# A 2-layer gMLP/mLSTM decoder step: where one weight split stands on VectorE, and five transposes instead of six for a head's values

## The chip, the core and the metric

The kernel runs on one core of one Trainium2 chip. The metric is device time in microseconds of one execution of the whole program. TensorE (PE in the profile) multiplies matrices and transposes; VectorE (DVE), ScalarE (ACT) and GpSimd (POOL) do the elementwise work; SyncE (SP) issues all DMAs of this kernel, in one queue. Matmul results go to PSUM, which has eight banks of 512 float32 columns on 128 partitions; everything else is in SBUF.

## The reference

One inference step of a decoder with two layers, on 256 prompt tokens and on 8 sequences of 8 new sample tokens (64 tokens), together 320 columns. Each layer is a mixer and a gated MLP with a causal convolution; layer 0 mixes by chunked spatial gating, layer 1 by an mLSTM with 8 heads, key width 128 and value width 256. The change touches layer 1, whose mixer computes per head

```python
p = x @ w_in                       # q, k (through a causal convolution and silu), v, o, gates
sc = einsum('bhtd,bhsd->bhts', qc, kc) * w_intra
num = w_inter[..., None] * einsum('bhtd,bhde->bhte', qc, C) + einsum('bhts,bhse->bhte', sc, vc)
h = num / maximum(abs(den), exp(-m_t))[..., None]
C_new = decay[..., None, None] * C + einsum('bhsd,bhse->bhde', kg, vc)
hn = (h - mean(h)) * rsqrt(var(h) + EPS) * gn_g
y = (sigmoid(o_pre) * hn) @ w_out
```

The outputs are y for all tokens, and the new states, among them C for the prompt and for each of the eight sample sequences.

## The kernel before

**Precision.** Every float32 operand of a matmul is split into a high part that TensorE's fast float32 form (fp32r) holds exactly enough, and a low part, the rest: names end in `h` and `l`. A product takes three matmuls: high by high, low by high, high by low. For each weight chunk of 128 x 1024 (`raw`), ScalarE writes the high part `wh` (L154) and VectorE the low part `wl = raw - wh` (L155).

**Weights.** A list fixes the order of all weight chunks. `take` (called once for each chunk that TensorE uses) sees to it that four chunks further on are being loaded (`AHEAD`), and that one chunk further on is split (`SPLIT_AHEAD`), by calling `prefetch(n, m)`: load until n chunks are loaded, split until m are split. `raw` has four buffers, `wh` and `wl` three each. `block` multiplies eight chunks of rows into one PSUM tile `pm`; in layer 1 all products with `wh` come first, then those with `wl`.

**Order.** Matmuls and transposes are pinned to program order (`mm`, `tr`). The instructions of the other engines are placed by a scheduler, which may move an instruction ahead of others of its engine where its inputs allow; `tc.issue_after(x)` keeps what is issued inside it behind instruction x. PSUM is used through two pools, `psm` with three banks (tag `pm`) and `psa` with five (tag `pa`).

**The heads.** The loop over `h` at the end of `layer_b` interleaves head `h` with the rest of head `h - 1`. For `h` from 1 on TensorE runs the six blocks of head `h` (q, k, v, v, o, o), and between them, of head `h - 1`: the product of the queries with the old states (`inter`, tile `num`, with the split states `Ch` and `Cl`), the numerator (`numer`), the new prompt state (`state_prompt`), and in four pieces the new sample states (`state_sample`, tile `pcs`, then `C` on VectorE, then the store `out_Cs`); then the scores of head `h` (`scores`, tile `psc`). After the last block come

- `finish(h - 1)`: for each half `e` of the 256 value columns, three transposes of the normalised output `hn` into `phn`, then `y_b = (tanh + 1) * phn` on VectorE (L1027), then its high part `yhb` on ScalarE (L1029) and its low part `ylb` on VectorE (L1030), with the gain;
- `state_sample(h - 1, 3)`;
- `k_nat(h)`: three transposes of k into `pk`, from which `kgs` (sample) and `kgh`, `kgl` (prompt) are made; `kgs`, masked per sequence on GpSimd, is `kgz`;
- `v_nat(h)`: transposes of v into `pv`, see below;
- `inter(h, 0)`, whose first matmul opens a new PSUM tile `num`; then the splits of two more states.

With `rows_in(h)` at the top of the loop the load of `Mb` (one row of gate weights, spread over the partitions) is issued; `w`, the exponentials of the gates, read it on ScalarE (L811). From head 4 on the loop also runs the first half of the output projection (`early`), which adds blocks of matmuls with little work on the other engines. `o_b` (L1013) is the scaled o block, and `qk_epi` makes `bpad`, the convolution `bcv` (one instruction on ScalarE, three on VectorE), `bth`, `qs` and their parts `qh`, `qhl`, `kh`, `khl`.

**The values.** v comes out of the blocks with channels on partitions and tokens on columns, one `pm` for each half `e`. `v_epi` copies it to `vTb`: 320 columns, and the 64 sample columns once more behind them, so that columns 256 to 383 hold the sample's tokens twice. `v_nat` transposes three groups of 128 columns of both halves, six transposes; in the third group the sample's 64 tokens so stand on partitions 0 to 63 and again on 64 to 127. ScalarE writes the high part `vh[:, t]` of each group from PSUM with the tokens' scale (L851), VectorE the low part (L854): for the prompt's two groups to `vl`, for the sample's to partitions 64 to 127 of `vh[:, 2]`, over the second copy, so that one matmul of 128 rows sums high and low. `vb` holds copies of that for the sequences 4 to 7 (L856, L857).

Of the kernel before, what the change touches and what calls it, by code (L numbers as in the profile page):

```python
# [10 lines left out]
F32 = mybir.dt.float32  # L11
F32R = mybir.dt.float32r
AF = mybir.ActivationFunctionType
ALU = mybir.AluOpType
MULT, ADD, SUB, MAX = ALU.mult, ALU.add, ALU.subtract, ALU.max

P = 128
EPS = 1e-6
TP = 256
NB, NS = 8, 8  # L20
T = TP + NB * NS
# [6 lines left out]
DV = 256  # L28
# [9 lines left out]
class Net:  # L38
# [597 lines left out]
    def layer_b(self):  # L636
        nc, tc, I, O = self.nc, self.tc, self.I, self.O
# [4 lines left out]
        with ExitStack() as ctx:  # L642
            lp = ctx.enter_context(tc.tile_pool(name="lb", bufs=1))
# [109 lines left out]
            S = [dict() for _ in range(NH)]  # L753
# [31 lines left out]

            def v_epi(h, j, ps):
                vT = lp.tile([P, 384], F32, tag="vT", name="vTb", bufs=2)
                nc.scalar.copy(vT[:, :T], ps[:, :T])
                nc.scalar.copy(vT[:, T:384], ps[:, TP:T])
                S[h].setdefault("vT", []).append(vT)  # L790

            def rows_in(h):
                mb = hp.tile([P, 392], F32, tag="Mb", name="Mb", bufs=2)
                nc.sync.dma_start(mb, I["rows"][h:h + 1, :].to_broadcast([P, 392]))
                S[h]["rows"] = mb
# [45 lines left out]
            def v_nat(h):  # L841
                s = S[h]
                pv = [self.psa.tile([P, 512], F32, tag="pa", name="pv") for _ in range(2)]
                dsts = [pv[t // 2][:, (t % 2) * DV:] for t in range(3)]
                for t in range(3):
                    for e in range(2):
                        self.tr(dsts[t][:, e * P:(e + 1) * P], s["vT"][e][:, t * P:(t + 1) * P], self.ident)
                for t in range(3):
                    dst = dsts[t]
                    sc = self.rc[:, t:t + 1]  # L850
                    nc.scalar.activation(vh[:, t, :DV], dst[:, :DV], AF.Copy, scale=sc)  # L851

                    r, out = (slice(0, P), vl[:, t, :DV]) if t < 2 else (slice(64, P), vh[64:, t, :DV])
                    nc.vector.scalar_tensor_tensor(out, dst[r, :DV], sc[r], vh[r, t, :DV].bitcast(F32), op0=MULT, op1=SUB)  # L854

                nc.scalar.copy(vb[:, :DV], vh[:, 2, :DV])  # L856
                nc.scalar.copy(vb[:32, :DV], vh[32:64, 2, :DV])  # L857
# [48 lines left out]
            def state_split(h, i):  # L906
                C0 = S[h]["C"][i]
                Ch = lp.tile([P, 2, CW], F32R, tag="Ch", name="Ch", bufs=3)
                Cl = lp.tile([P, 2, CW], F32R, tag="Cl", name="Cl", bufs=3)
                nc.scalar.copy(Ch, C0)  # L910
                low = nc.vector.tensor_tensor(Cl, C0, Ch.bitcast(F32), op=SUB)  # L911
                S[h].setdefault("Cs", []).append((Ch, Cl))
                return low

            def inter(h, i):

                s = S[h]
                if i == 0:
                    s["num2"] = self.psa.tile([P, 512], F32, tag="pa", name="num")
                d = s["num2"][:, :CW]  # L920
                Ch, Cl = s["Cs"][i]
                for u in range(2):
                    b = 2 * i + u
                    lhs = Qz[:, b * P:(b + 1) * P]
                    mm(d, lhs, Ch[:, u, :], b == 0, False)
                    mm(d, lhs, Cl[:, u, :], False, False)
# [57 lines left out]
            def state_prompt(h):  # L984
                s = S[h]
                kgh, kgl, _, _ = s["kg"]
                pc = self.psa.tile([P, 512], F32, tag="pa", name="pCp")
                for t in range(2):
                    mm3(pc[:, :CW], kgh[:, t, :], kgl[:, t, :], vh[:, t, :], vl[:, t, :], t == 0, t == 1)

                Cp = hp.tile([P, CW], F32, tag="Cp", name="Cp", bufs=1)
                nc.scalar.copy(Cp, pc[:, :CW])
                nc.sync.dma_start(O["Cp"][h], Cp)
# [21 lines left out]
                nc.scalar.activation(th, o, AF.Tanh, scale=0.5)  # L1015
                S[h].setdefault("o", []).append(th)

            def finish(h):
                s = S[h]
                yh = hp.tile([P, 2, T], F32R, tag="yhb", name="yhb", bufs=6)  # L1020
                yl = hp.tile([P, 2, T], F32R, tag="ylb", name="ylb", bufs=6)
                for e in range(2):
                    pt = self.psa.tile([P, 512], F32, tag="pa", name="phn")
                    for t in range(3):
                        self.tr(pt[:, t * P:(t + 1) * P], hn[:, t, e * P:(e + 1) * P], self.ident)
                    y = self.tp.tile([P, T], F32, tag="yf", name="y_b", bufs=2)
                    nc.vector.scalar_tensor_tensor(y, s["o"][e], 1.0, pt[:, :T], op0=ADD, op1=MULT)  # L1027
                    g = gnh[:, 2 * h + e:2 * h + e + 1]
                    nc.scalar.activation(yh[:, e, :], y, AF.Copy, scale=g)  # L1029
                    nc.vector.scalar_tensor_tensor(yl[:, e, :], y, g, yh[:, e, :].bitcast(F32), op0=MULT, op1=SUB)  # L1030
                    Y[2 * h + e] = (yh[:, e, :], yl[:, e, :])

            def early(h, r):
                for m in self.EARLY_OUT.get((h, r), ()):
                    self.residual(m, self.block(8, lambda k: Y[k]))
# [5 lines left out]
            vh = hp.tile([P, 3, CW], F32R, name="vh")  # L1041
            vl = hp.tile([P, 2, CW], F32R, name="vl")
# [18 lines left out]
            def blk():  # L1061
                return self.block(KD, self.x_rhs)
# [19 lines left out]
            for h in range(NH):  # L1082
                if h:
                    rows_in(h)
                    qk_epi(h, 0, blk())
                    early(h, 0)
                    if h == 1:
                        inter(0, 0)
                        state_split(0, 3)
                    inter(h - 1, 1)  # L1090
                    qk_epi(h, 1, blk())
                    for i in (2, 3):
                        inter(h - 1, i)
                    numer(h - 1)
                    early(h, 1)
                    ps = blk()
                    with self.behind_split():
                        stats(h - 1)
                    v_epi(h, 0, ps)
                    state_prompt(h - 1)  # L1100
                    made = state_sample(h - 1, 0)
                    early(h, 2)
                    v_epi(h, 1, blk())
                last = h == NH - 1
                if last:
                    with tc.issue_after(made.ins):
                        made = normed(h - 1)
                    states(h, made)
                if h:
                    made = state_sample(h - 1, 1)  # L1110
                    if not last:
                        with tc.issue_after(made.ins):
                            normed(h - 1)
                scores(h)
                early(h, 3)
                if h and not last:
                    o_epi(h, 0, blk())
                if last:
                    finish(h - 1)
                    begin(0)  # L1120
                if h:
                    for i in (2, 3) if last else (2,):
                        state_sample(h - 1, i)
                if last:
                    begin(1)

                    self.prefetch(0, self.used + 2)
                early(h, 4)
                if h and not last:
                    states(h, made)  # L1130
                if h and not last:
                    o_epi(h, 1, blk())
                if h and not last:
                    finish(h - 1)
                    state_sample(h - 1, 3)
                k_nat(h)
                v_nat(h)
                if h:
                    inter(h, 0)
                    for i in (2, 3):  # L1140
                        low = state_split(h, i)
                else:
                    with tc.issue_after(self.parts[0].ins), tc.issue_after(self.parts[1].ins):
                        state_split(0, 2)
                early(h, 5)
            nc.sync.dma_start(O["b_state"], nst)

            h = NH - 1
# [8 lines left out]
            ps = blk()  # L1157
# [14 lines left out]
            for m in range(KD):  # L1172
                ps = part.get(m)
                if ps is None:
                    ps = self.block(8, lambda k: Y[8 + k])
# [154 lines left out]
```

## Time and profile before

| | us |
|---|---|
| median of three runs | 953.72 |
| lowest, highest | 953.01, 955.09 |
| the profiled execution, its own time | 954.62 |
| its span, from the first to the last instruction | 952.9 |
| TensorE busy in the span | 945.6 |
| VectorE busy | 695.6 |
| ScalarE busy | 530.5 |

The granted TensorE clock was 0.999 in the profiled execution. Layer 1's mixer lies between 424 and 714 us. In the time line of a row the first number is the start in us from the span's start, the second the length from the first start to the last end of the instructions that the row puts together (`x6` is six of them); a bracket tells how long the engine had been idle, and what it had waited for. Consecutive instructions of one engine overlap a little, so starts lie closer together than lengths.

### The profile page before, as it was taken

To read this page: it belongs to the slowest core of one execution; us is meant where nothing else is said; L and a number is where in the kernel's file an instruction comes from. 1 tells how busy PE (TensorE), PEld (TensorE's weight loads), DVE (VectorE), ACT (ScalarE), POOL (GpSimd) and SP (SyncE) were. 2 spreads that over 40 slices of the span, in tenths; PEclk is the share of its full clock that TensorE was granted. 3 is DMA by queue.
4 is the path that set the end of the run, shared out by engine and by line. 5 is a ranking of instruction groups with operands and counts; after the bars stand their busy time and mean duration, and the time that the engine had idled before them with its cause. 6 is when DMAs were issued, how large, how long until landed. Compare 5 with 4: busy or idle time off the path is not lost.

```text
span 952.9 us, 17084 instructions
## 1 busy us (share of the span) xinstructions
PE 945.6 (99%) x6420; PEld 932.8 (98%) x6420; DVE 695.6 (73%) x1324; ACT 530.5 (56%) x978; POOL 117.6 (12%) x291
## 2 busy tenths in 40 slices
PE   9999999999999999999999999999999999999997
PEld 8889999999999999999999999999999999999997
DVE  6766976577777764559999998788888777775443
ACT  7557543454554443348877767666765544554342
POOL 3200000010000000014442312303001000000000
PEclk9999999999999999999999999999999999999999
DMA  8643346544444455565465756654474444445541
GB/s 272 209 153 133 130 134 190 175 140 150 153 156 147 141 159 156 146 215 176 155 201 185 219 174 207 198 183 133 132 250 144 156 148 145 151 150 152 145 138 56
DMA packets 55238, 156.15 MB, mean 164 GB/s; under 512 B 7492, under 2 KB 13132, under 8 KB 55156
## 3 DMA queue, kind: packets, MB, share of 16 engines
q1 hardware_dynamic: 55156, 155.06, 51.2%
q8 instruction: 51, 0.84, 0.3%
q14 instruction: 31, 0.25, 0.1%
HBM read 143.05 MB, written 11.99 MB: 163 GB/s over the span
## 4 chain that ended last, share of the span: by engine, by line
PE 93%; DVE 3%; ACT 1%; issue 1%; POOL 0%; DMA 0%; SPq 0%; POOLq 0%; ACTq 0%
PE pm L54 80%; PE pv_a L54 6%; PE num L54 2%; PE pmix L54 1%; PE pcs L54 1%; PE pCp L54 1%; PE phn L57 0%; PE psc L54 0%; DVE wl L155 0%; PE pv L57 0%; PE pc L54 0%; ACT wh L154 0%; PE pg L54 0%; DVE Cl L911 0%; DMA raw<-in_a_wv 0%
## 5 line engine op out<-in xcount | busy, mean ns | idle before, releaser
L154 ACT CAST wh<-raw 128x1024 fp32r<-128x1024 f32 (+3 forms) x256 | 256.7, 1004 | 270.8 <-PE pm L54 141.5
L155 DVE TENSOR_TENSOR wl<-raw,wh 128x1024 fp32r<-128x1024 f32 (+3 forms) x256 | 298.8, 1168 | 121.0 <-ACT wh L154 116.5
L54 PE MATMUL pm<-xh,wh 128*128 128x320 f32 x1216 | 372.2, 311 | 0.0
L54 PE MATMUL pm<-xl,wh 128*128 128x320 f32 x1216 | 370.3, 309 | 0.0
L54 PE MATMUL pm<-xh,wl 128*128 128x320 f32 x1216 | 321.2, 309 | 0.0
L54 PEld LDWEIGHTS pm<-xl,wh 128*128 128x128 f32 x1216 | 228.4, 188 | 0.2
L54 PEld LDWEIGHTS pm<-xh,wh 128*128 128x128 f32 x1216 | 228.3, 188 | 0.2
L54 PEld LDWEIGHTS pm<-xh,wl 128*128 128x128 f32 x1216 | 214.5, 188 | 0.0
L54 PE MATMUL pm<-yh_f,wh 128*128 128x320 f32 x352 | 108.8, 309 | 0.0
L54 PE MATMUL pm<-yl_f,wh 128*128 128x320 f32 x352 | 108.8, 309 | 0.0
L54 PE MATMUL pm<-yh_f,wl 128*128 128x320 f32 x352 | 108.8, 309 | 0.0
L54 PEld LDWEIGHTS pm<-yh_f,wh 128*128 128x128 f32 x352 | 66.1, 188 | 0.0
L54 PEld LDWEIGHTS pm<-yl_f,wh 128*128 128x128 f32 x352 | 66.1, 188 | 0.0
L54 PEld LDWEIGHTS pm<-yh_f,wl 128*128 128x128 f32 x352 | 66.1, 188 | 0.0
L532 DVE SCALAR_TENSOR_TENSOR fcv<-fpad,vecs,fcv 128x336 f32<-128x336 f32 x88 | 49.5, 565 | 2.1 <-ACT fcv L530 0.6
L54 PE MATMUL pm<-yh_a,wh 128*128 128x320 f32 x128 | 39.6, 310 | 0.0
L54 PE MATMUL pm<-yh_a,wl 128*128 128x320 f32 x128 | 39.5, 309 | 0.0
L54 PE MATMUL pm<-yl_a,wh 128*128 128x320 f32 x128 | 39.5, 309 | 0.0
L534 ACT ACTIVATE fgl<-fcv 128x256 f32<-128x256 f32 x44 | 18.3, 415 | 37.9 <-DVE fcv L532 37.8
L54 PE MATMUL pm<-yhb,wh 128*128 128x320 f32 x128 | 38.2, 311 | 0.0
L54 PE MATMUL pm<-ylb,wh 128*128 128x320 f32 x128 | 37.9, 309 | 0.0
L304 DVE TENSOR_TENSOR xT<-pm,xT 128x320 f32<-128x320 f32 x39 | 19.0, 488 | 24.7 <-PE pm L54 24.5
(289 smaller groups left out, 1366.5 us busy)
## 6 DMA issues: line engine op xcount, KB each, us to landing
raw<-in_f_up SPq DMA_DIRECT2D x88, 512.0 KB, 3.3
raw<-in_b_win SPq DMA_DIRECT2D x48, 512.0 KB, 4.1
raw<-in_f_dn SPq DMA_DIRECT2D x32, 448.0 KB, 3.4
C<-in_C SPq DMA_DIRECT2D x32, 258.0 KB, 3.9
out_Cs<-C SPq DMA_DIRECT2D x32, 258.0 KB, 4.0
raw<-in_a_win SPq DMA_DIRECT2D x16, 512.0 KB, 3.2
raw<-in_a_wo SPq DMA_DIRECT2D x16, 512.0 KB, 4.0
raw<-in_f_dn SPq DMA_DIRECT2D x16, 512.0 KB, 3.6
```

What stands on the lines that cost most here:

```text
L54: self.pin(self.nc.tensor.matmul(out, lhsT, rhs, start=start, stop=stop, skip_group_check=skip))
L154: self.last_split = self.hold(nc.scalar.copy(wh[:, :kn, :], raw[:, :kn, :]))
L155: self.last_low = nc.vector.tensor_tensor(wl[:, :kn, :], raw[:, :kn, :], wh[:, :kn, :].bitcast(F32), op=SUB)
L304: self.nc.vector.tensor_tensor(x, ps[:, :T], x, op=ADD)
L532: nc.vector.scalar_tensor_tensor(cv, pd[:, i:i + NC], self.vec(w + i * KF), cv, op0=MULT, op1=ADD)
L534: nc.scalar.activation(gl[:, :TP], cv[:, :TP], AF.Gelu_apprx_tanh)
```

## The change

Two parts of `layer_b`.

The first: `finish` gets an argument `ahead`, which is true for heads 0 to 5. The six transposes and both `y_b` are issued first, with `yhb` and `ylb` of both halves behind them; and where `ahead` is true the split of the chunk after the next one is asked for right behind the second `y_b`, which is one chunk earlier in the program than `take` would ask for it.

```diff
-            def finish(h):
+            def finish(h, ahead=False):
...
+                ys = []
                 for e in range(2):
...
-                    y = self.tp.tile([P, T], F32, tag="yf", name="y_b", bufs=2)
-                    nc.vector.scalar_tensor_tensor(y, s["o"][e], 1.0, pt[:, :T], op0=ADD, op1=MULT)
+                    ys.append(self.tp.tile([P, T], F32, tag="yf", name="y_b", bufs=2))
+                    made = nc.vector.scalar_tensor_tensor(ys[e], s["o"][e], 1.0, pt[:, :T], op0=ADD, op1=MULT)
+                if ahead:
+                    with tc.issue_after(made.ins):
+                        self.prefetch(0, self.used + 2)
+                for e, y in enumerate(ys):
                     g = gnh[:, 2 * h + e:2 * h + e + 1]
...
-                    finish(h - 1)
+                    finish(h - 1, True)
```

The second: for heads 1 to 7 `v_epi` copies the prompt's 256 columns to `vTb` and the sample's 64 to one tile `vS`, half 0 to its columns 0 to 63 and half 1 to 64 to 127. One transpose of `vS` puts the sample's tokens of half 0 on partitions 0 to 63 and those of half 1 on 64 to 127 of the same 128 columns. From there the high and the low part are made by two instructions each, of 64 partitions and 128 columns. Head 0 keeps the six transposes.

```diff
             def v_epi(h, j, ps):
...
-                nc.scalar.copy(vT[:, :T], ps[:, :T])
-                nc.scalar.copy(vT[:, T:384], ps[:, TP:T])
+                if h:
+                    nc.scalar.copy(vT[:, :TP], ps[:, :TP])
+
+                    if not j:
+                        S[h]["vS"] = lp.tile([P, P], F32, tag="vS", name="vS", bufs=1)
+                    nc.scalar.copy(S[h]["vS"][:, 64 * j:64 * j + 64], ps[:, TP:T])
+                else:
...
             def v_nat(h):
...
-                for t in range(3):
+                both = "vS" in s
+                for t in range(2 if both else 3):
                     for e in range(2):
                         self.tr(dsts[t][:, e * P:(e + 1) * P], s["vT"][e][:, t * P:(t + 1) * P], self.ident)
...
+                if both:
+                    self.tr(dsts[2][:, :P], s["vS"], self.ident)
...
+                lo = slice(64, P)
+                if both:
+                    for e, r in enumerate((slice(0, 64), lo)):
+                        c, sc = slice(e * P, (e + 1) * P), self.rc[r, 2:3]
+                        nc.scalar.activation(vh[:64, 2, c], dsts[2][r, :P], AF.Copy, scale=sc)
+                        nc.vector.scalar_tensor_tensor(vh[lo, 2, c], dsts[2][r, :P], sc, vh[:64, 2, c].bitcast(F32), op0=MULT, op1=SUB)
+                else:
...
```

More of the change, by code (lines that the diff above doesn't have):

```diff
@@ L787, in v_epi @@
                 vT = lp.tile([P, 384], F32, tag="vT", name="vTb", bufs=2)
-                nc.scalar.copy(vT[:, :T], ps[:, :T])
-                nc.scalar.copy(vT[:, T:384], ps[:, TP:T])
+                if h:
[4 more added lines that the diff above has]
+                else:
+                    nc.scalar.copy(vT[:, :T], ps[:, :T])
+                    nc.scalar.copy(vT[:, T:384], ps[:, TP:T])
                 S[h].setdefault("vT", []).append(vT)
@@ L844, in v_nat @@
                 dsts = [pv[t // 2][:, (t % 2) * DV:] for t in range(3)]
-                for t in range(3):
+                both = "vS" in s
+                for t in range(2 if both else 3):
                     for e in range(2):
                         self.tr(dsts[t][:, e * P:(e + 1) * P], s["vT"][e][:, t * P:(t + 1) * P], self.ident)
-                for t in range(3):
-                    dst = dsts[t]
+                if both:
+                    self.tr(dsts[2][:, :P], s["vS"], self.ident)
+                for t in range(2):
                     sc = self.rc[:, t:t + 1]
-                    nc.scalar.activation(vh[:, t, :DV], dst[:, :DV], AF.Copy, scale=sc)
-                    r, out = (slice(0, P), vl[:, t, :DV]) if t < 2 else (slice(64, P), vh[64:, t, :DV])
-                    nc.vector.scalar_tensor_tensor(out, dst[r, :DV], sc[r], vh[r, t, :DV].bitcast(F32), op0=MULT, op1=SUB)
+                    nc.scalar.activation(vh[:, t, :DV], dsts[t][:, :DV], AF.Copy, scale=sc)
+                    nc.vector.scalar_tensor_tensor(vl[:, t, :DV], dsts[t][:, :DV], sc, vh[:, t, :DV].bitcast(F32), op0=MULT, op1=SUB)
+                lo = slice(64, P)
[5 more added lines that the diff above has]
+                else:
+                    sc = self.rc[:, 2:3]
+                    nc.scalar.activation(vh[:, 2, :DV], dsts[2][:, :DV], AF.Copy, scale=sc)
+                    nc.vector.scalar_tensor_tensor(vh[lo, 2, :DV], dsts[2][lo, :DV], sc[lo], vh[lo, 2, :DV].bitcast(F32), op0=MULT, op1=SUB)
                 nc.scalar.copy(vb[:, :DV], vh[:, 2, :DV])
```

## The prediction

> **What bounds the kernel now.** I read the page first, then the busy time by stretch, then the waits of TensorE, then the timelines around those waits.
>
> ```profile
> span 952.9 us, 17084 instructions
> PE 945.6 (99%) x6420; PEld 932.8 (98%) x6420; DVE 695.6 (73%) x1324; ACT 530.5 (56%) x978; POOL 117.6 (12%) x291
> ```
>
> TensorE is busy for 945.6 of 952.9 us, so only work taken from TensorE, or a wait of TensorE, moves the end. The share of VectorE is a mean; by stretch, in the mLSTM layer, it looks different:
>
> ```profile
> core 0: us, PE busy (x) PEld busy (x) DVE busy (x) ACT busy (x) POOL busy (x), PEclk, DMA share, GB/s
> 478.00:506.30 28.30, 28.30 (x205) 28.29 (x206) 27.29 (x66) 21.51 (x50) 8.25 (x9) 1.00 0.62 198
> 506.30:534.90 28.60, 28.60 (x211) 28.59 (x210) 27.06 (x66) 22.00 (x52) 8.41 (x13) 1.00 0.62 192
> 534.90:563.30 28.40, 28.40 (x209) 28.39 (x208) 26.91 (x65) 21.78 (x51) 8.36 (x13) 1.00 0.62 197
> 563.30:602.10 38.80, 38.80 (x279) 38.79 (x279) 31.49 (x71) 24.87 (x54) 7.49 (x13) 1.00 0.66 211
> ```
>
> The rows are heads 2, 3, 4 and 5. TensorE never pauses there, but in heads 2 to 4 VectorE has 1.0 to 1.5 us free of 28.4, in head 5 7.3 us (the output projections run there, which give VectorE little). The only wait of TensorE in the layer stands at the end of head 1 (first row: the list of waits, with total, times and longest; the others: the timeline, with start and length):
>
> ```profile
> PE num L54 <- DVE y_b L1027: 0.3, 1, 0.3
> 476.92 0.82 PE L57 MATMUL pv<-ident,vTb 128*128 128x128 f32 x6
> 477.99 0.39 PE L54 MATMUL num<-Ch,Qz 128*128 128x258 f32 x1 [0.26 <-DVE y_b L1027]
> 475.15 0.86 DVE L1007 SCALAR_TENSOR_TENSOR C<-C,dec,pcs 128x258 f32<-128x258 f32 x2
> 475.94 1.21 DVE L155 TENSOR_TENSOR wl<-raw,wh 128x1024 fp32r<-128x1024 f32 x1
> 477.07 0.47 DVE L1013 TENSOR_TENSOR o_b<-pm,rb 128x320 f32<-128x320 f32 x1
> 477.47 0.87 DVE L1027 SCALAR_TENSOR_TENSOR y_b<-th_o,phn 128x320 f32<-128x320 f32 x2
> ```
>
> `num` takes the PSUM bank of the first `phn`, which the first `y_b` reads; and a weight's low part (1.21 us) stands on VectorE ahead of `o_b` and `y_b`.
>
> **The change part by part.**
>
> *Transposes.* Heads 1 to 7 issue five `pv` transposes instead of six.
>
> ```profile
> L57 PE MATMUL pv<-ident,vTb x48: 272/273/273, 448.1 to 672.6; 128*128 128x128 f32 x48
> L851 ACT ACTIVATE vh<-pv,rc x24: 459/472/496, 450.4 to 674.2; 128x256 fp32r<-128x256 f32 x24
> L854 DVE SCALAR_TENSOR_TENSOR vh<-pv,rc,vh x8: 490/491/492, 454.9 to 673.8; 64x256 fp32r<-64x256 f32 x8
> L886 ACT ACTIVATE kgh<-pk,cols x16: 365/368/371, 455.3 to 676.2; 128x128 fp32r<-128x128 f32 x16
> L887 DVE SCALAR_TENSOR_TENSOR kgl<-pk,cols,kgh x16: 335/341/351, 456.2 to 677.2; 128x128 fp32r<-128x128 f32 x16
> ```
>
> Six take 0.82 us from first start to last end, one lasts 0.273, so they start (0.82 − 0.273)/5 = 0.109 us apart. Seven fewer: 7 × 0.109 = 0.77 us, all on TensorE's own line, which has no gap there.
>
> *What replaces them.* ScalarE's `vh` of the sample (0.472) becomes two of 64x128, VectorE's low part (0.491) two as well. Such a form does not occur; the nearest rows are the 128x128 `kgh` (0.368) and `kgl` (0.341). From above: +0.26 on ScalarE, +0.19 on VectorE a head. From below nothing, since consecutive instructions overlap by some 0.08 us (two `y_b` take 0.87, not 0.95). I take +0.1 each: hidden where the engine has time (head 5 and on), and at heads 2 to 4 taken from the 1.0 to 1.5 us. The `vTb` copy of 320 columns becomes 256, no longer than before. [...]
>
> *The low part behind `y_b`.* In the built program's order the low part for the block after next stands behind both `y_b` at the end of heads 1 to 6, no longer ahead of them. Its `wh` on ScalarE is not moved past them. At head 1 `o_b` can start at 475.94, the first `y_b` at 476.34, and ends by 476.82. The last of six transposes starts at 476.92 + 5 × 0.109 = 477.47, so `num` could start at 477.58; it starts at 477.99. The wait of 0.41 goes, with 0.65 us to spare. No such wait stands at later heads, so nothing more is gained there:
>
> ```profile
> 504.81 0.49 DVE L1013 TENSOR_TENSOR o_b<-pm,rb 128x320 f32<-128x320 f32 x1 [0.60 <-PE phn L57]
> 533.56 0.88 DVE L1027 SCALAR_TENSOR_TENSOR y_b<-th_o,phn 128x320 f32<-128x320 f32 x2
> 534.68 0.36 PE L54 MATMUL num<-Ch,Qz 128*128 128x258 f32 x1
> ```
>
> At the end of head 2 VectorE has to wait for TensorE even with the low part in front. At the end of head 3 the first `y_b` ends at 533.56 + 0.48 = 534.04, 0.64 us ahead of `num`: that is the cover there.
>
> *What is late next.* The low part now runs after `y_b`, where VectorE does not idle, so what stands behind it (two `ylb`, two `C` updates, `kgs`, `vl`) is late. The second `C` update releases the DMA that stores the state, and on SP's queue the load of `Mb` (the row of gate weights) stands behind that store:
>
> ```profile
> 507.50 0.48 DVE L1007 SCALAR_TENSOR_TENSOR C<-C,Mb,pcs 128x258 f32<-128x258 f32 x1
> 508.00 0.33 SPq L903 DMA_DIRECT2D C<-in_C  x1
> 508.42 0.39 SPq L1008 DMA_DIRECT2D out_Cs<-C  x1
> 508.86 0.42 SPq L794 DMA_DIRECT2D Mb<-rows  x1
> DMA to landing us min/median/max: 4.3/4.7/5.5
> 514.42 1.04 ACT L811 ACTIVATE w<-Mb,cols 128x256 f32<-128x256 f32 x3 [1.53 <-DMA Mb<-rows]
> 542.79 1.04 ACT L811 ACTIVATE w<-Mb,cols 128x256 f32<-128x256 f32 x3 [1.56 <-DMA Mb<-rows]
> ```
>
> The `C` update ends at 507.98; with the low part ahead of it, 1.13 us from start to start (475.94 to 477.07), it ends near 509.1. So `Mb` is issued near 509.55 (+0.7) and, at 4.3 to 5.5 us, lands at 513.9 to 515.05. ScalarE already waits for it (1.53 and 1.56 us in heads 3 and 4). In the new order the first `w` stands ahead of the second `kgh`, both `vb`, `bcv` and the next `wh`; before, all of these but that `wh` were ahead of it:
>
> ```profile
> 510.58 0.37 ACT L886 ACTIVATE kgh<-pk,cols 128x128 fp32r<-128x128 f32 x1
> 510.84 0.40 ACT L856 CAST vb<-vh 128x256 fp32r<-128x256 f32 x1
> 512.21 0.68 ACT L768 ACTIVATE bcv<-bpad,vecs 128x344 f32<-128x344 f32 x1
> 515.37 1.04 ACT L154 CAST wh<-raw 128x1024 fp32r<-128x1024 f32 x1
> 516.31 1.14 ACT L910 CAST Ch<-C 128x516 fp32r<-128x516 f32 x2
> 517.35 0.49 ACT L772 ACTIVATE bth<-bcv 128x344 f32<-128x344 f32 x1
> 511.40 0.34 DVE L887 SCALAR_TENSOR_TENSOR kgl<-pk,cols,kgh 128x128 fp32r<-128x128 f32 x1
> 516.44 1.23 DVE L155 TENSOR_TENSOR wl<-raw,wh 128x1024 fp32r<-128x1024 f32 x1 [0.35 <-ACT wh L154]
> 517.88 0.43 DVE L774 SCALAR_TENSOR_TENSOR qs<-bth,bcv 128x256 f32<-128x256 f32 x1 [0.21 <-ACT bth L772]
> 519.70 0.42 DVE L312 TENSOR_TENSOR qhl<-qs,qh 128x256 fp32r<-128x256 f32 x1 [0.68 <-ACT qh L312]
> ```
>
> So `kgh`, done at 510.95 before, comes 0.8 us after the landing (0.41 of `w`, 0.37 of its own): 514.7 to 515.85. VectorE needed 3.42 us from the end of `C` to the second `kgl` (507.98 to 511.40); in the new order a low part stands ahead of that `kgl` too, so it gets there near 509.1 + 3.42 + 1.13 = 513.65 and waits 1.05 to 2.2 us where it did not before. ScalarE, from `kgh` at 514.7 (landing 4.7 us after issue), has `kgh`, two `vb`, two `bcv`, a `wh`, two `w` and a `Ch` ahead of `bth`: 0.27 + 0.61 + 1.16 + 0.95 + 0.54 + 0.53 = 4.06 us with the overlap of some 0.1 taken off each, so `bth` starts near 518.8 and `qs` near 519.2 instead of 517.88. Behind it the old wait of 0.68 for `qh` is covered (two more instructions stand ahead of `qhl` now): VectorE is late by 1.3 − 0.68 = 0.6 us, or by all of 1.3 if nothing is covered. Head 3 has 0.64 − 0.11 of cover, head 4 the same path, no cover left and one transpose less. Given back over both: 2 × 0.6 − 0.53 + 0.11 = 0.8 us, at most 2 × 1.3 − 0.42 = 2.2, at least nothing, if `Mb` lands early. I take 1.0, nearer the middle of these and its median landing. Heads 5 and 6 have some 7 us free.
>
> *Other queues.* On SP one weight load changes places with a state load in most heads; it is issued four blocks ahead (4 × 3.5 us) and is there in some 4. On GpSimd the masks `kgz` wait for the later `kgs`, and are read three blocks on: both hidden.
>
> **The sum.** −0.77 − 0.41 + 1.0 = −0.2 us. The profiled execution took 954.62 us (1.7 around its span), 0.9 above the median of the runs; its result is 954.4, and from the median 953.72 it is 953.5 us, no change that can be told.
>
> **The rivals.**
>
> 1. *A clean gain.* The second `C` update, and with it `Mb`, keeps its time, or the cover of 0.64 holds at both heads. For it: TensorE had not one wait in heads 2 to 7. Against it: 1.0 to 1.5 us free in 28.4, and ScalarE already waiting for `Mb`. Time: 953.72 − 1.18 = 952.5.
> 2. *Slower: VectorE becomes the bound at heads 3 and 4.* `Mb` lands 5.5 us after its later issue, as it did at 508.86 to 514.4, in each head. It decides from a landing near 514.1, where `kgl` waits 1.25 us: less the 0.68 that it covers, this uses up the 0.53 of head 3. At 515.05 `kgl` waits 2.2 us, and VectorE is late by 1.5 us a head: 2 × 1.5 − 0.42 = 2.6, and some 0.8 where head 4 hands its lateness on to the `C` update and so to the `Mb` of head 5: +3.4 − 1.2 = +2.2, so 955.9. Against it: the landing in head 4 was faster, and from head 5 on VectorE catches up.
> 3. *The change doesn't do what it says.* The wait at 477.99 goes over to another reader of the bank, and only the transposes count while heads 3 and 4 still give 1.0 back: 953.72 − 0.77 + 1.0 = 953.9. Against it: only the two `y_b` read `phn`. [...]
>
> **How the numbers follow.** Forecast 0.45, clean gain 0.25, slower 0.2, the third 0.1. About 0.2% (1.9 us) is what a measurement of this kernel can tell from no change. Its own spread (953.01 to 955.09 in three runs) lets a median move by some 0.6. Range: 952.1, the clean gain less a part of that spread, to 955.4, which takes in the full 2.2 given back, its spread, and the near part of the slower case. Faster than 951.8 needs more than the whole gain: 0.07. Slower than 955.6 holds most of the second rival: 0.17. Within: 0.76.
>
> **What would show it.** Right: `pv` transposes 41 instead of 48 in number; no wait of `num` for `y_b` at the end of head 1; the `w` of heads 3 and 4 still waiting for `Mb`, with VectorE's `kgl` waiting for `kgh` behind it; and short waits of `num` for `y_b` at the ends of heads 3 and 4, some 1 us together. No wait there means the first rival. Wrong: waits of TensorE in heads 5 to 7, or a `Mb` issued no later than before.

## The result: slower by 4 to 5 us

| | before | changed |
|---|---|---|
| median, us | 954.06 (953.01 to 955.94) | 958.98 (957.13 to 960.14) |
| ratio of the times, 95% interval | | 1.0048 [1.0038, 1.0058] |
| the profiled execution, its own time | 954.62 | 959.83 |
| its span | 952.9 | 958.1 |

The forecast was 953.5 us, in a range of 952.1 to 955.4. The changed kernel is outside it, slower by more than twice what a measurement of this kernel can tell from no change. A second set of runs of the same kernel gave 957.83 us against 953.86, a ratio of 1.0044 [1.0029, 1.0058]. (The ratios are estimated from all runs of both kernels and are not the quotients of the two medians.)

The page of the changed kernel, its head and the busy times:

```profile
span 958.1 us, 17099 instructions
PE 946.8 (99%) x6413; PEld 933.6 (97%) x6413; DVE 698.5 (73%) x1331; ACT 530.2 (55%) x985; POOL 117.3 (12%) x291
```

TensorE has seven matmuls fewer, the transposes. It is busy for 1.2 us longer all the same, and the span has grown by 5.2 us. The busy time by stretch says where (columns as before; `PEclk` is the granted clock):

```profile
478.00:506.30 28.30, 28.30 (x208) 28.29 (x207) 27.69 (x66) 21.84 (x52) 7.70 (x9) 1.00 0.59 187
506.30:534.90 28.60, 25.93 (x174) 25.75 (x174) 23.65 (x60) 18.35 (x45) 8.58 (x13) 0.94 0.55 179
534.90:563.30 28.40, 26.26 (x192) 26.07 (x191) 23.63 (x59) 18.50 (x45) 8.59 (x13) 1.00 0.50 161
563.30:602.10 38.80, 38.49 (x275) 38.17 (x274) 35.64 (x79) 27.07 (x61) 8.04 (x13) 1.00 0.68 216
```

In head 2 TensorE is as full as before. In heads 3 and 4 it stands for 2.7 and 2.1 us, and VectorE and ScalarE do *less* in the same time than before: no engine is overloaded, all of them wait. In head 3 the granted clock is lower too (0.94). The list of TensorE's waits:

```profile
PE pcs L54 <- ACT vh L879: 4.8, 2, 2.7
PE num L54 <- DVE y_b L1046: 0.3, 1, 0.3
```

Two waits of `pcs` make 4.8 us. The timeline of the changed kernel, first the end of head 1, then head 3 around the first of these waits, engine by engine:

```profile
477.20 0.36 PE L54 MATMUL num<-Ch,Qz 128*128 128x258 f32 x1
510.97 0.61 ACT L928 CAST Ch<-C 128x516 fp32r<-128x516 f32 x1
516.60 0.51 ACT L818 ACTIVATE w<-Mb,cols 128x256 f32<-128x256 f32 x1 [5.02 <-DMA Mb<-rows]
517.02 0.35 ACT L904 ACTIVATE kgh<-pk,cols 128x128 fp32r<-128x128 f32 x1
...
518.69 1.05 ACT L154 CAST wh<-raw 128x1024 fp32r<-128x1024 f32 x1
...
522.17 0.40 ACT L879 CAST vh<-vh 32x256 fp32r<-32x256 f32 x1
517.40 0.35 DVE L905 SCALAR_TENSOR_TENSOR kgl<-pk,cols,kgh 128x128 fp32r<-128x128 f32 x1 [3.85 <-ACT kgh L904]
519.76 0.28 PE L54 MATMUL pCp<-vh,kgl 128*128 128x258 f32 x1
522.72 0.48 PE L54 MATMUL pcs<-vh,kgz 128*128 128x258 f32 x2 [2.67 <-ACT vh L879]
```

The wait at the end of head 1 is gone (`num` at 477.20 has no bracket; the 0.3 us in the list stand at the end of head 4). In head 3 ScalarE stands 5.02 us in front of `w`, until `Mb` lands. VectorE waits 3.85 us for the `kgh` behind `w`, as the prediction said in kind. But TensorE is stopped by something else: by the copy of 32 rows of `vh` (L879, `v_first`, which `stats` issues for the head before). It stands further behind in ScalarE's queue, and the first `pcs` of the sample states reads it. In the kernel before the same two instructions stand like this:

```profile
518.83 0.41 ACT L861 CAST vh<-vh 32x256 fp32r<-32x256 f32 x1
520.80 0.40 PE L54 MATMUL pcs<-vh,kgz 128*128 128x258 f32 x2
```

The copy ended at 519.24, 1.56 us ahead of its reader: that was the cover of head 3.

`Mb` is late because of SP's queue. Its timeline in the changed kernel, start and length of each issue, and the `C` updates on VectorE in the last row:

```profile
504.62 0.38 SPq L1026 DMA_DIRECT2D out_Cs<-C  x1
509.23 0.33 SPq L921 DMA_DIRECT2D C<-in_C  x1
509.66 1.04 SPq L127 DMA_DIRECT2D raw<-in_b_win  x1
510.79 0.38 SPq L1026 DMA_DIRECT2D out_Cs<-C  x1
511.22 0.42 SPq L801 DMA_DIRECT2D Mb<-rows  x1
507.30 0.86 DVE L1025 SCALAR_TENSOR_TENSOR C<-C,Mb,pcs 128x258 f32<-128x258 f32 x2
```

and the waits of SP between 500 and 520 us, the first of the list:

```profile
SPq L921 <- DMA out_Cs<-C: 13.1, 3, 4.5
```

A state load `C<-in_C` overwrites the buffer that the store ahead of it reads, so it waits for that store's landing, and everything behind it on SP waits too (13.1 us in three such waits between 500 and 520; before, 10.7 in three). Before, the load went out at 508.00; here at 509.23: 1.23 us. Then a weight load, which stood elsewhere before, sits between it and the last store and takes 1.04 us to issue: 1.13 us more. So `Mb` leaves at 511.22 instead of 508.86 (+2.36), and lands near 516.6. What did *not* make it late: both `C` updates were done at 508.16.

### The profile page after: what moved, and what is told of

It is laid out like the page before. It is cut to its first block, busy times and chain, and to the rows that moved or that the text cites. A ratio compares the mean times of both kernels' runs of the same rounds, so it can differ in the third digit from the quotient of the medians.

```text
span 958.1 us, 17099 instructions
## 1 busy us (share of the span) xinstructions
PE 946.8 (99%) x6413; PEld 933.6 (97%) x6413; DVE 698.5 (73%) x1331; ACT 530.2 (55%) x985; POOL 117.3 (12%) x291
## 4 chain that ended last, share of the span: by engine, by line
PE 95%; DVE 2%; ACT 1%; issue 1%; DMA 1%; POOL 0%; POOLq 0%; SPq 0%
PE pm L54 82%; PE pv_a L54 6%; PE num L54 2%; PE pmix L54 1%; PE pcs L54 1%; DMA Mb<-rows 1%; PE psc L54 1%; PE pCp L54 0%; PE phn L57 0%; PE pc L54 0%; PE pw L54 0%; PE pv L57 0%; PE pg L54 0%; DVE Cl L929 0%; ACT wh L154 0%
```

## The experiments

Theory Q (queue): `Mb` is late on SP, ScalarE stands in front of `w`, and what TensorE needs waits behind it. Theory E (engines): the changed work is too much for VectorE and ScalarE in heads 2 to 4, wherever `Mb` lands. Each kernel was timed beside the kernel before.

| kernel | median, us | before, us | ratio, 95% interval |
|---|---|---|---|
| transpose of `vS` alone | 954.97 | 953.84 | 1.0005 [0.9996, 1.0013] |
| low part behind `y_b` alone | 956.99 | 953.84 | 1.0026 [1.0017, 1.0035] |
| changed, `Mb` a head earlier | 952.78 | 953.84 | 0.9983 [0.9974, 0.9992] |
| before, `Mb` a head earlier | 953.97 | 953.84 | 0.9996 [0.9987, 1.0005] |
| before, `Mb` late | 962.09 | 953.75 | 1.0084 [1.0070, 1.0098] |
| `vS` alone, `Mb` a head earlier | 953.46 | 953.75 | 0.9995 [0.9987, 1.0004] |
| low part alone, `Mb` a head earlier | 954.00 | 953.75 | 1.0003 [0.9994, 1.0012] |
| changed, copy of `vh` on GpSimd | 958.70 | 953.75 | 1.0048 [1.0036, 1.0061] |
| changed, `Mb` on GpSimd's queue | 955.93 | 953.86 | 1.0018 [1.0010, 1.0027] |
| changed, again | 957.83 | 953.86 | 1.0044 [1.0029, 1.0058] |
| changed, `Mb` late | 967.95 | 953.86 | 1.0142 [1.0128, 1.0156] |
| changed, `w` behind `vb` and `bcv` | 953.15 | 954.09 | 0.9987 [0.9978, 0.9996] |
| the same, and `Mb` on GpSimd's queue | 953.20 | 954.09 | 0.9991 [0.9983, 1.0000] |

**The parts alone.** First, `finish` with its body and its call as before (the call alone is shown), so that only the transposes are changed:

```diff
-                    finish(h - 1, True)
+                    finish(h - 1)
```

> Only the second part of the change: one transpose of vS for heads 1 to 7, with finish as before. Theory Q (the changed kernel lost its time because Mb is issued 2.36 us later on SP's queue, lands at 516.58 instead of 514.40, and ScalarE then stands 5 us in front of w while the sample rows of vh, which pcs needs, wait behind it): here the low part stands ahead of y_b again, so nothing makes the C update late, but a weight load still stands ahead of a state store in front of Mb. If Mb of heads 3 and 4 is issued no more than 0.7 us later than before, TensorE has no wait for vh and the time is 954.06 - 0.77 = 953.3 us; a wait for vh of over 1 us is expected only together with a wait of w for Mb of over 3 us. Theory E (the rival: the split vh instructions and the moved work are too much for VectorE and ScalarE in heads 2 to 4, wherever Mb lands): 954 to 956 us, with waits of TensorE in heads 3 and 4 though w waits for Mb no longer than the 1.5 us of before.

TensorE's waits in this kernel:

```profile
PE num L54 <- DVE y_b L1045: 1.1, 3, 0.4
```

and `w` of head 3 in its timeline:

```profile
514.46 0.51 ACT L818 ACTIVATE w<-Mb,cols 128x256 f32<-128x256 f32 x1 [2.51 <-DMA Mb<-rows]
```

Neither theory had this. `Mb` was issued at 508.55, no later than before, but landed 5.9 us later, at 514.46. `pcs` does not wait; yet there is no gain. `num` waits for `y_b` at the ends of heads 1, 3 and 4: at heads 3 and 4 these are the short waits that the prediction had placed there. The time is the one that theory E forecast, but not with its condition, since `w` waits for `Mb` longer than the 1.5 us of before; the same kernel with an early `Mb`, below, decides.

Second, `v_epi` as before, so that six transposes stay and only `finish` is changed (the edit is the first diff of the change, alone):

> Only the first part of the change: finish with the low part behind y_b, six transposes as before. Both theories: the 0.41 us wait of num at the end of head 1 goes. Theory Q: on SP's queue a weight load stands ahead of the state store in front of Mb here as well, so Mb is issued 1 to 2.4 us later than before; where ScalarE's wait in front of w grows to over 3 us, TensorE waits for vh after it, and the time is 955 to 958 us; if the wait stays under 3 us, 953.7 us. Theory E: the work added on VectorE and ScalarE by the split vh is not there, so there is no loss: 953.7 us, whatever Mb does.

TensorE's waits in this kernel, and `w` of head 3 and two later instructions in its timeline:

```profile
PE psc L54 <- ACT kh L312: 1.3, 1, 1.3
```

```profile
516.39 0.51 ACT L811 ACTIVATE w<-Mb,cols 128x256 f32<-128x256 f32 x1 [2.30 <-DMA Mb<-rows]
519.85 0.42 DVE L957 TENSOR_TENSOR ns<-num,ns 64x258 f32<-64x258 f32 x1 [2.02 <-ACT ns L956]
525.97 0.30 ACT L312 CAST kh<-qs 128x128 fp32r<-128x128 f32 x1 [1.17 <-DVE qs L774]
```

Most of the loss comes with this part, which adds no work: theory E falls here. Theory Q's bound of 3 us was wrong, too: a wait of 2.30 us in front of `w` is enough, and it is `kh` that `psc` waits for. `kh` is not held in ScalarE's queue: VectorE stands 2.02 us for `ns`, which ScalarE makes behind `w`, so its `qs` is late, and ScalarE waits 1.17 us for that. This is the way over VectorE on which the prediction had looked. The profiled execution (955.85 us) shows one wait of 1.3 us; where the rest of the 3 us in the median comes from is not shown.

**`Mb` earlier.** In the changed kernel the row is loaded one head earlier:

```diff
-                mb = hp.tile([P, 392], F32, tag="Mb", name="Mb", bufs=2)
+                mb = hp.tile([P, 392], F32, tag="Mb", name="Mb", bufs=3)
...
-                    rows_in(h)
+                    for g in ((1, 2) if h == 1 else (h + 1,)):
+                        if g < NH:
+                            rows_in(g)
```

> The changed kernel with the load of Mb for a head issued one head earlier (three buffers for Mb instead of two); nothing else is changed, though the w of a head then also run earlier on ScalarE. Theory Q: no wait of w for Mb, no wait of pcs for vh in heads 3 and 4, no drop of the clock behind it; the whole gain of the change is seen: 954.06 - 0.77 - 0.41 = 952.9 us (952.4 to 953.4). Theory E: the work stays, so the time stays at 957 to 959 us, with TensorE still waiting in heads 3 and 4.

952.78 us: the whole gain of the change, and TensorE has no wait in the layer. It has the lowest median of all kernels here, and the interval of its ratio lies below 1, where that of the changed kernel lies above. The same edit in the kernel before:

> Control: the kernel before with the load of Mb one head earlier. Both theories: the 1.5 us for which ScalarE waits for Mb in heads 3 and 4 cost TensorE nothing in the kernel before (it has no wait there), so the time stays at 954.1 us within 0.6. If it falls by 1 us or more, an earlier Mb is a gain by itself, and the gain of the third kernel is not that of the change.

953.97 us, no change, so the gain above is the change's own: 952.78 − 953.97 = −1.19, where the prediction's two terms of gain make −1.18. That they agree so closely is luck: the interval of the ratio is 0.9 us wide to either side. Each part with the early `Mb`:

> The second part of the change alone (one transpose of vS), with the load of Mb one head earlier. Theory Q: the 0.77 us of the seven transposes, less the wait of num at the end of head 1, which grows from 0.42 to about 0.54 us: 953.84 - 0.77 + 0.11 = 953.2 us. If waits of num for y_b at the ends of heads 3 and 4 stay as in the first experiment (1.1 us of waits in three places), VectorE's order and not Mb makes them, and the time is 953.2 + 0.8 = 954.0 us.

> The first part of the change alone (low part behind y_b, six transposes), with the load of Mb one head earlier. Theory Q: the wait of 0.41 us at the end of head 1 goes, no wait of psc for kh as in the second experiment: 953.84 - 0.41 = 953.4 us. Theory E: the later C updates and kgl still cost time without the late Mb, 955 us or more.

953.46 and 954.00 us, both within the spread of the kernel before. In the first, only the wait of `num` at the end of head 1 is left (0.4 us), so those of heads 3 and 4 in the first experiment came from `Mb`. In the second TensorE has no wait left in the layer, but the median shows none of the 0.41 us: medians do not separate so little. The parts can't be priced apart by these times, but the profiles can do it, by the start of each head's first `psc` against the kernel before: with `finish` alone TensorE gains 0.51 us from head 1 to head 2 and keeps it; with `vS` alone it gains nothing there and then 0.09 to 0.12 us a head.

**`Mb` late, and nothing else.** In the kernel before, the load of `Mb` is put behind the next state load on SP (`C_in` is the last load of `state_in`, which `states` no longer calls for these heads):

```diff
-                    rows_in(h)
+                    state_in(h)
+                    with tc.issue_after(S[h]["C_in"].ins):
+                        rows_in(h)
```

> Neither part of the change: the kernel before, with one DMA moved on SP's queue. The load of Mb stands behind the state load that follows it, which waits for the landing of the store ahead (512.55 in the kernel before). Theory Q: Mb is issued near 513.0 instead of 508.86 and lands at 517.3 to 518.5 instead of 514.40. In the kernel before vh is copied by 519.24 and pcs starts at 520.80, so 1.56 us are spare; from the start of w to that copy 3.3 us remain when wh and a Ch are taken out (they stand elsewhere in this order), so the copy ends at 520.6 to 521.8: a wait of pcs of 0 to 1.0 us in heads 3 and 4, and kh behind it late by 1 to 3 us, so that psc waits. Time 955 to 958 us, with TensorE waiting in heads 3 and 4 for ScalarE. Theory E (the loss comes from the changed instructions themselves): 954 us, no wait.

TensorE's waits in this kernel, and `Mb` and `w` of head 3 in its timeline:

```profile
PE pcs L54 <- ACT vh L861: 5.4, 3, 2.2
```

```profile
517.63 0.42 SPq L794 DMA_DIRECT2D Mb<-rows  x1
522.29 1.04 ACT L811 ACTIVATE w<-Mb,cols 128x256 f32<-128x256 f32 x3 [5.22 <-DMA Mb<-rows]
```

962.09 us, with no instruction added or taken away (the scheduler moves some on ScalarE and VectorE): a late `Mb` gives the same waits for the same copy. It is more than expected, because I worked from head 3 alone: the wait begins in head 2, delays the stores, and so puts the `Mb` of head 3 at 517.63 instead of 513.0.

**The last link.** The changed kernel with `v_first` on GpSimd:

```diff
-                nc.scalar.copy(vh[32:64, 2, :DV], vh[:32, 2, :DV])
+                nc.gpsimd.tensor_copy(vh[32:64, 2, :DV], vh[:32, 2, :DV])
```

> The changed kernel, Mb as late as in it, but the copy of the sample rows of vh, which pcs waits for, is made by GpSimd instead of ScalarE. If pcs is held by the place of that copy in ScalarE's queue behind w, bcv and bth (theory Q's last link), the copy starts behind GpSimd's second mask of w (520.11 to 520.43 in the changed kernel) and ends near 520.9 instead of 522.57: the wait of pcs at head 3 falls from 2.67 to about 1.0 us, and in head 4 alike. kh, which is as late as before, then holds psc for what is left, as it did by 1.3 us in the second experiment: time 955.5 to 958 us, with waits of psc for kh. If the wait of pcs stays at 2 us or more, it is not that copy that holds it.

TensorE's waits in this kernel:

```profile
PE pcs L54 <- POOL vh L879: 1.8, 2, 0.9
PE pm L54 <- DVE kgl L905: 1.0, 1, 1.0
...
PE psc L54 <- ACT kh L312: 0.7, 2, 0.3
PE num L54 <- DVE y_b L1046: 0.6, 2, 0.3
```

The two waits of `pcs` fall from 4.8 to 1.8 us, so that copy held it. The time stays at 958.70: `kh`, `kgl` and `y_b` are late as well, and take the place. One link eased does not help here while ScalarE as a whole is late.

**Late on SP, or misplaced on ScalarE?** First `Mb` on another queue, at the same place of the program:

```diff
-                nc.sync.dma_start(mb, I["rows"][h:h + 1, :].to_broadcast([P, 392]))
+                nc.gpsimd.dma_start(mb, I["rows"][h:h + 1, :].to_broadcast([P, 392]))
```

> The changed kernel with the load of Mb issued on GpSimd's queue instead of SP's, at the same place of the program and with the same two buffers. Theory Q: GpSimd is idle there (10.4 us ahead of kgz at 508.70), so Mb is issued as soon as the C update that last reads its buffer is done (508.16), near 508.3 instead of 511.22, and lands at 512.6 to 514; ScalarE waits for it 2 us or less instead of 5.0; no wait of pcs for vh in heads 3 and 4; 952.8 to 954 us. If the work of the change and not SP's order makes Mb late, the issue stays near 511 and the time near 959 us.

`Mb` of head 3 on GpSimd, and `w` of head 4, in this kernel's timeline:

```profile
508.48 0.63 POOL L801 DMA_DIRECT2D Mb<-rows  x1 [10.40 <-DVE C L1025]
...
542.29 0.51 ACT L818 ACTIVATE w<-Mb,cols 128x256 f32<-128x256 f32 x1 [1.93 <-DMA Mb<-rows]
```

The issue came where expected, and head 3 is whole (table below). But the time is 955.93, not 954 or less: in head 4 the landing took 5.5 us, ScalarE stood 1.93 us, and TensorE lost 1.5 us from the first `psc` of head 4 to that of head 5. The kernel before stands there for 1.56 us and loses nothing. So the late issue is not all. What differs is what stands behind `w`: in the kernel before `kgh`, `vb` and `bcv` are ahead of it. Second, ScalarE's order alone is put back, with SP's order as in the changed kernel (`vb_made` and `cv_made` are the second `vb` and the first `bcv`):

```diff
+                    with tc.issue_after((self.vb_made if h else self.cv_made).ins), tc.issue_after(self.cv_made.ins):
                         nc.scalar.activation(w[:n, o:o + c1 - c0], pb[:n, c0:c1], AF.Exp, scale=-1.0, bias=colsT[:n, t, h:h + 1])
```

> The changed kernel with only ScalarE's order held: w stands behind both vb and the first bcv of the head, as in the kernel before (the wh between them too). SP's order is that of the changed kernel, so Mb is still issued at 510.4 to 511.2 in head 3 and lands at 514.6 to 516.6. Theory Q1 (the late Mb is the loss): w starts as late as in the changed kernel, pcs and psc wait as there, 956 to 959 us. Theory Q2 (the place of w in ScalarE's queue turns the late Mb into a loss): kgh, vb, bcv and wh are done before w, kgl does not wait 3.85 us, and behind w only w itself, ns, bcv, bth stand ahead of the copy of vh, which ends 2.6 us after the landing instead of 6.0, by 517.2 to 519.2, before pcs wants it (519.9): no wait of pcs, 952.8 to 954.5 us.

Head 3 in this kernel's timeline, `Mb` on SP and then ScalarE:

```profile
509.63 0.91 SPq L803 DMA_DIRECT2D Mb<-rows  x1
513.42 1.05 ACT L154 CAST wh<-raw 128x1024 fp32r<-128x1024 f32 x1
514.42 1.04 ACT L821 ACTIVATE w<-Mb,cols 128x256 f32<-128x256 f32 x3
516.84 0.41 ACT L882 CAST vh<-vh 32x256 fp32r<-32x256 f32 x1
```

953.15 us: the whole gain, with `Mb` still issued later than in the kernel before (the issue ends at 510.54, there at 509.28) and TensorE 1 us ahead of it. ScalarE works through `kgh`, `vb`, `bcv` and `wh` while `Mb` is under way, and does not stand for it at all; the copy of `vh` ends 2.83 us after `w` begins, where the changed kernel needs 5.97. `Mb` is not as late here as in the first profile of the changed kernel (the issue ends at 511.64), but nearly as late as in its second (510.84, below), where `pcs` waits 0.86 us in this head. Both together:

> As the one before it, and Mb issued on GpSimd's queue as in the ninth experiment, with two buffers. Q1 and Q2 together (both the issue of Mb and the place of w as good as before): no wait of TensorE for ScalarE in heads 3 and 4, 952.7 to 953.5 us. If a loss of over 1 us stays here, a third cause is left: the changed work on VectorE and ScalarE itself.

953.20 us, nothing left for a third cause.

**The changed kernel again, and with a later `Mb`** (the edit of the fifth experiment):

> The changed kernel once more, for its time on this chip and for the granted clock behind the pauses of TensorE. Both theories: 957 to 960 us, pcs waiting 2.2 to 2.8 us in heads 3 and 4. If a pause of 2.8 us lowers the granted clock, the matmuls behind the first pause are again about 0.12 us further apart for some 3 us in the profile; if the drop seen once was chance, the pitch stays.

> The changed kernel with Mb behind one more state load on SP's queue, as in the fifth experiment. Theory Q: ScalarE waits for Mb longer than the 4.0 to 5.2 us of that experiment, pcs waits 2 to 4 us in heads 2 to 5, and the time is 960 to 966 us. If pauses lower the granted clock, those of over 2.8 us are followed by a stretch with a granted clock under 1.00, and those of under 2.4 us are not.

TensorE's waits in the repeated changed kernel, and `Mb` and `w` of head 3 in its timeline:

```profile
PE pcs L54 <- ACT vh L879: 2.4, 2, 1.6
```

```profile
510.41 0.43 SPq L801 DMA_DIRECT2D Mb<-rows  x1
514.58 0.51 ACT L818 ACTIVATE w<-Mb,cols 128x256 f32<-128x256 f32 x1 [3.19 <-DMA Mb<-rows]
```

This execution took 956.48 us. There `Mb` was issued 0.8 us earlier and landed 4.2 us after its issue, not 5.4, and the waits of `pcs` (0.86 and 1.59 us) are half as long, shorter than expected. So the two profiled executions of this kernel differ by when a small load lands, and its spread is wide (956.5 to 961.2 us in this set). With no pause near 2.8 us, this profile says nothing on the clock. With `Mb` late on top the kernel takes 967.95 us, more than the 966 expected; its waits of `pcs` are 2.39, 3.45, 1.97 and 2.35 us in heads 2 to 5. The first `psc` of each head, against the profile of the kernel before (start less start, us), sums up; what stands in the column of head 1 comes from ahead of the change and is no effect of it:

| head | 1 | 2 | 3 | 4 | 5 | 7 |
|---|---|---|---|---|---|---|
| changed | −0.18 | −0.81 | +3.53 | +5.81 | +6.38 | +6.14 |
| changed, again | −0.39 | −1.01 | −0.03 | +2.37 | +2.91 | +2.68 |
| changed, `Mb` on GpSimd's queue | −0.14 | −0.76 | −0.87 | −0.62 | +0.85 | +0.96 |
| changed, `Mb` a head earlier | −0.32 | −0.94 | −1.04 | −1.14 | −1.25 | −1.45 |
| changed, `w` behind `vb` and `bcv` | −0.42 | −1.03 | −1.14 | −1.24 | −1.34 | −1.57 |
| before, `Mb` late | −0.11 | +2.13 | +5.06 | +6.92 | +7.39 | +7.36 |

## Why the prediction was wrong

- **Transposes, −0.77: right.** 34 and 7 `pv` transposes stand in the profile, and the two changed kernels without waits (fourth and fifth row of the table) gain 0.10 to 0.11 us a head from head 2 to head 5.
- **The wait of `num` at the end of head 1, −0.41: right.** From head 1 to head 2 the changed kernel gains 0.63 us, where this wait and one transpose make 0.52; with `finish` alone it is 0.51, so the wait was worth 0.5.
- **The halves of `vh`, "+0.1 each": too low, and harmless.** They cost nearly what the bound from above said: 2 × 0.358 − 0.472 = +0.24 us on ScalarE, 2 × 0.350 − 0.491 = +0.21 on VectorE a head, from these groups:

```profile
L867 ACT ACTIVATE vh<-pv,rc 64x128 fp32r<-64x128 f32 x14 | 5.0, 358 | 0.2
L868 DVE SCALAR_TENSOR_TENSOR vh<-pv,rc,vh 64x128 fp32r<-64x128 f32 x14 | 4.9, 350 | 0.5
```

- **"`Mb` is issued near 509.55 (+0.7)": wrong.** It was issued at 511.22 (+2.36). The prediction made the `C` update late and took nothing else. That update was done at 508.16, 0.18 us later than before and not 1.13; most of the difference is the 0.81 us by which TensorE was ahead in head 2. SP itself made the delay, by a store's landing and a weight load. The prediction had set that exchange aside as hidden, because the weights come in time. They do; but SP issued in order, and it was `Mb` that stood *behind* the exchanged load, which made 1.13 of its 2.36 us.
- **"Given back, +1.0 (0 to 2.2)": the step that failed.** The prediction saw the new order on ScalarE (`w` ahead of `kgh`, `vb`, `bcv`, `wh`) and followed its lateness over to VectorE, to `y_b`, with a cover of 0.64 us. It did not follow the same queue down to its own next output that TensorE reads. From `w` to the end of the `vh` copy there are 5.97 us, and `pcs` wants the copy at 519.89 (0.13 behind the last `pCp`). Even with the latest landing that the prediction worked out, 515.05, the copy would have ended at 521.0, 1.1 us too late; in the repeated run `Mb` landed at 514.58, and `pcs` waited 0.86 us. In the profile of before, the cover of this copy could be read, 1.56 us. The runs showed the place (GpSimd making the copy) and the cause (`w` put behind).
- **The sum after.** The pauses in heads 3 and 4 are 2.83 and 2.30 us from start to start (less the 0.12 to 0.13 that lie between such matmuls anyway), and 0.47 at the end of head 4; about 1.5 more went with the clock (below): 7.1 us in place of the +1.0. Less the gains of 1.18 this is +5.9, near the +6.3 from head 1 to head 7 in the table; the other 0.4 is not accounted for. The span grew by 5.2, also because SP issued the last stores of `y` in 0.7 us less (2.36 instead of 3.07).
- **The rivals.** The slower one (955.9) had the late `Mb`, but went through VectorE, and was too short by the same step. The clean gain (952.5) is what the changed kernel does, within the noise, once `w` is held or `Mb` is loaded a head earlier. The third falls: no other reader holds `num` at the end of head 1.

What stays open: why the scheduler places `w` there in the changed kernel; why a small load takes 4.2 us to land in one execution and 5.4 in another; and why the store's landing took 4.6 us instead of 3.3 (a weight load of 512 KB was issued just ahead of it there, and behind it before; that was not tried).

## What to carry to other kernels

When an instruction that waits for a DMA moves up in an engine's queue, list everything behind it, and look up for each the first reader on the bounding engine and the slack to it in the profile; the shortest slack decides, not the chain that comes to mind. On a DMA queue that issues in order, as SP's did here, ask of each exchange who stands behind it, since one load that waits for a store's landing holds small, urgent loads too (`Mb`, here, for 1.23 us more than before). A loss by order can be cured by order: one line that holds `w`, or a load asked for a head earlier, turned +4 to 5 us into −1.

## What was not expected of the hardware

A pause of TensorE cost more than its length here: behind the 2.83 us of head 3 about 1.5 us more went. The busy time by stretch of the changed kernel, up to the pause of head 3 and behind it:

```profile
513.00:522.70 9.70, 7.04 (x53) 6.85 (x52) 5.06 (x11) 5.98 (x15) 3.13 (x8) 1.00 0.46 162
522.70:527.40 4.70, 4.68 (x22) 4.70 (x23) 4.70 (x20) 3.94 (x13) 0.21 (x1) 0.64 0.37 134
```

The same of the changed kernel with the later `Mb`, behind its pauses of 2.55, 3.61 and 2.51 us:

```profile
493.80:498.00 4.20, 4.13 (x29) 4.06 (x29) 4.08 (x16) 4.02 (x14) 0.21 (x1) 1.00 0.02 6
...
527.00:530.50 3.50, 3.50 (x14) 3.50 (x15) 3.38 (x10) 3.50 (x10) 0.21 (x1) 0.51 0.00 0
...
597.90:602.20 4.30, 4.24 (x19) 4.27 (x20) 4.30 (x15) 3.24 (x10) 0.21 (x1) 0.60 0.34 124
```

And matmuls of 320 columns from its timeline, where the second stretch begins and where it ends:

```profile
527.42 0.47 PE L54 MATMUL pm<-xh,wh 128*128 128x320 f32 x1
527.69 0.47 PE L54 MATMUL pm<-xl,wh 128*128 128x320 f32 x1
...
530.56 0.31 PE L54 MATMUL pm<-xh,wh 128*128 128x320 f32 x1
530.71 0.32 PE L54 MATMUL pm<-xl,wh 128*128 128x320 f32 x1
```

Behind pauses of 2.83, 3.61 and 2.51 us the granted clock was 0.64, 0.51 and 0.60 over 4.70, 3.50 and 4.30 us. An estimate from these: if it was a half for a time, as in nearly all of the second stretch, and full for the rest, the half lasted some 3.4 us in each. Behind the first two the matmuls start 0.27 us apart instead of 0.15, so that by the same estimate about 1.5 us are lost each time (0.12 of every 0.27 us in 3.4); at the first the table has it too, +3.53 less −0.81 from head 2 to head 3, 1.5 more than the pause. Behind the pause of 2.55 us the clock was full (29 matmuls in 4.2 us, granted 1.00), and so it was behind pauses of 2.38 us (`Mb` late in the kernel before: granted 1.00 over 4.3 us) and 2.30 us (head 4 of the changed kernel: 1.00 over 4.2 us). Why 2.51 us lowered the clock and 2.55 us did not, no run here shows.
